# Decayed scores of HGRN and GLA in 64-row tiles of the array, written to two PSUM banks

## Chip, cores and metric

The kernel runs on one core of a Trainium2 chip. The metric is the device time of one execution in microseconds, as the median of several runs. A profiled execution of the same program gives the trace. TensorE's matmuls (PE) and its weight loads (PEld) are shown apart; VectorE is DVE, ScalarE ACT, GpSimd POOL, the DMA-issuing engine SP.

## What is computed

Two layers of a decoder. In each, one input projection feeds four groups of heads (retention, HGRN2, GLA, RWKV-7), their outputs go through one output projection, and cross-attention into 256 memory rows follows. It is done for a prompt of 2048 rows and for 8 x 8 sample rows. The change concerns HGRN2 and GLA, which are this recurrence (S is the state of one head, g the log of a decay per key channel):

```
def chunked_gated_linear(q, k, v, log_g, s0):
    """S_t = diag(exp g_t) S_{t-1} + k_t v_t^T, o_t = S_t^T q_t, evaluated chunkwise."""
    ...
    diff = b[:, :, :, None, :] - b[:, :, None, :, :]
    decay = jnp.where(causal, jnp.exp(jnp.minimum(diff, 0.0)), 0.0)
    scores = jnp.sum(qf[:, :, :, None, :] * kf[:, :, None, :, :] * decay, axis=-1)
    o = (jnp.einsum('bhjm,bhmv->bhjv', scores, vf)
         + jnp.einsum('bhjk,bhkv->bhjv', qf * jnp.exp(b), S))
```

HGRN has 4 heads of 64 key channels, GLA 4 heads of 32. All is float32.

## The kernel before

The prompt goes through each layer in four blocks of 512 rows. In a block come, in the order of the code: dense projections (groups of 12 or 24 matmuls, PSUM pool `psd`), RWKV in four units of 128 rows on the PSUM pools `psa` and `psc` in turn, GLA and HGRN in two half blocks of 256 rows each on the pool `psb` (two banks), retention, the gates (again dense groups), the output projection, cross-attention. A program orders the instructions of each engine once, before the run, by priorities that follow the code's order and the table `PRI`; `held` lifts eleven of twelve matmuls of a run so that a group stays together. Each engine then works through its own list in that order, so a matmul that waits holds up all that stand behind it.

`dyadic` (lines 670 to 740) makes the decayed scores of a half block. Scores between rows of one chunk of 128 are split by levels s = 1, 2, 4, ... 64: at level s, pairs of neighbouring runs of s rows are handled, the earlier run as keys, the later as queries. Between levels the keys of the earlier runs and the queries of the later runs are multiplied in place by the decay over the other run (`k_step`, `q_step`), so that each level is a plain product. The keys `k` lie with 128 channels on the partitions, which are two heads of HGRN (`NG` = 2, twice, `NC` = 2) or four of GLA (`NG` = 4, `NC` = 1). A matmul over all 128 partitions would add the heads up; so `apart` writes, for every product, `NG` copies of the level's queries into a tile `qx2` (two buffers), each masked to one head's channels (`hm2`, `hm4`). In the trace this tile is `qx`. `products` then takes 64 columns of `k` as weights and the masked copies as moving columns, into one PSUM bank of `psb`. The result is merged into the score tile `sT` by a multiplication with a mask (the two products of level 1) or by `copy_predicated` (levels 2 to 32, line 727); level 64 goes by ScalarE. `qk` of GLA shows as `dn_qk`, HGRN's queries and keys as `dn_hq` and `dn_hf`.

`outputs` (lines 605 to 668) multiplies queries by the state S and scores by the values into one bank, and updates S. GLA's state is a 128 x 256 tile: a 32 x 64 block for each of the four heads on the diagonal.

In the trace each float32 matmul of the code is two instructions, so a group that the code and the order give as 8 matmuls is 16 there.

Of the kernel before, what the change touches and what calls it, by code (L numbers as in the profile page):

```python
# [56 lines left out]
def shape_constants(seq, past):  # L57
    f = np.float32
    c = {}
# [43 lines left out]
    c["hm4"] = ((part // 32)[:, None] == np.arange(4)[None, :]).astype(f)  # L103
# [39 lines left out]
def decoder(ctx, tc, I, C, O):  # L143
# [461 lines left out]
    def outputs(seg, sT, v, qd, S, NG, NC, kT, tot, wp, eps, center, evac, state_out=None):  # L605

        P, nt = seg.P, seg.nt
        KD = 128 // NG
        if not seg.sample:
            po = PS("r").rearrange("p (t n) -> p t n", t=2)  # L610
            w = NG * 64
            for t in range(nt):
                for c in range(NC):
                    if center:
                        mm(po[:, t, c * w:(c + 1) * w], qd[:, c, t * 128:(t + 1) * 128], S[:, c, :], True, False)
                    else:
                        for e in range(2):
                            mm(po[64 * e:64 * e + 64, t, c * w:(c + 1) * w], qd[:, c, t * 128 + 64 * e:t * 128 + 64 * e + 64], S[:, c, :], True, False)
                    for g in range(NG):
                        h = c * NG + g  # L620
                        if center:
                            mm(po[:, t, h * 64:(h + 1) * 64], sT[:, t * NH + h].rearrange("p e n -> p (e n)"), v[:, t, h * 64:(h + 1) * 64], False, True)
                        else:
                            for e in range(2):
                                ep = slice(64 * e, 64 * e + 64)
                                mm(po[ep, t, h * 64:(h + 1) * 64], sT[:, t * NH + h, e, :], v[:, t, h * 64:(h + 1) * 64], False, True)
# [16 lines left out]
        for h in range(NH):  # L643
            c, g = divmod(h, NG)
            mm(pa[:SN, h * 64:(h + 1) * 64], sT[:SN, h, 0, :], v[:SN, 0, h * 64:(h + 1) * 64])
# [23 lines left out]

    def dyadic(seg, q, k, a, NG, NC, sT, wp):  # L670

# [3 lines left out]
        nh = P // 64  # L675
        m = nt * NC
        u = m * NG
        hm = K["hm%d" % NG]

        def apart(s, f):  # L680
            qx = wp.tile([128, NC, NG, n // 2], F32, name="qx2", tag="qx2", bufs=2)
            for c in range(NC):
                src = q[:, c].rearrange("p (b f s) -> p b f s", f=2, s=s)[:, :, f, :]
                shape = [128, NG, n // (2 * s), s]
                tt(V, qx[:, c].rearrange("p g (b s) -> p g b s", s=s), bc(src.unsqueeze(1), shape),
                   bc(hm.unsqueeze(2).unsqueeze(3), shape), ALU.mult)
            return qx

        def products(s, f):
            qx = apart(s, f)  # L690
            ps = PS("r")[:P, :u * 32].rearrange("p (i g n) -> p i g n", i=m, g=NG)
            for t in range(nt):
                for c in range(NC):
                    for e in range(nh):
                        b = t * nh + e
                        mm(ps[64 * e:64 * e + 64, t * NC + c], k[:, c, 64 * b:64 * b + 64], qx[:, c, :, 32 * b:32 * b + 32])
            out = sT[:P, :, 0, :].rearrange("p u (b f s) -> p u b f s", f=2, s=s)[:, :, :, f, :]
            return out, ps.rearrange("p i g (b s) -> p (i g) b s", s=s)
# [6 lines left out]
        def q_step(s, tot):  # L705
            qv = q.rearrange("p c (b f s) -> p c b f s", f=2, s=s)
            tv = tot.rearrange("p c (b f) -> p c b f", f=2)
            tt(V, qv[:, :, :, 1, :], qv[:, :, :, 1, :], bc(tv[:, :, :, 0:1], [128, NC, n // (2 * s), s]), ALU.mult)
# [4 lines left out]
        out, ps = products(1, 0)  # L713
        ev = K["I64"][:P].rearrange("p (b f) -> p b f", f=2)[:, :, 0:1]
        tt(V, out, ps, bc(ev.unsqueeze(1), [P, u, 32, 1]), ALU.mult)
        k_step(1, a)
        out, ps = products(1, 1)
        tt(V, out, ps, bc(K["pmask"][:P].unsqueeze(1).unsqueeze(3), [P, u, 32, 1]), ALU.mult)
        tt(V, q, q, a, ALU.mult)
        tot = q_step(1, a)  # L720
        for li, s in enumerate(seg.levels):
            if s == 1:
                continue
            if s < 64:
                out, ps = products(s, 1)
                mk = dmask[:P, li].rearrange("p (b s) -> p b s", s=s).unsqueeze(1)
                V.copy_predicated(out, bc(mk, [P, u, 32 // s, s]), ps)  # L727
            else:
                qx = apart(s, 1)
                A.activation(sT[64:128, :, 1, :], sT[64:128, :, 0, :], AF.Copy)  # L730
                G.memset(sT[64:128, :, 0, :], 0.0)
                ps = PS("r")[:, :NH * 64].rearrange("p (i g n) -> p i g n", i=NC, g=NG)
                for c in range(NC):
                    for t in range(nt):
                        mm(ps[64 * t:64 * t + 64, c], k[:, c, t * P:t * P + 64], qx[:, c, :, t * 64:(t + 1) * 64])
                for t in range(nt):
                    A.activation(sT[0:64, t * NH:(t + 1) * NH, 1, :], ps[64 * t:64 * t + 64].rearrange("p i g n -> p (i g) n"), AF.Copy)
            k_step(s, tot)
            tot = q_step(s, tot)
        return tot  # L740
# [28 lines left out]
    def R_gla(l, seg, st, d, on, wp):  # L769
# [16 lines left out]
        tot = dyadic(seg, qk[:, 0:1, :], qk[:, 1:2, :], a, 4, 1, sT, wp)  # L786
# [1209 lines left out]
```

## Time and profile before

| | us |
|---|---|
| median of 3 runs | 3726.42 |
| lowest, highest | 3723.85, 3737.66 |
| the profiled execution | 3730.45 |
| its span, first to last instruction | 3728.6 |

The profile is of one execution. Busy time counts an engine's instructions from start to end; matmuls overlap in the pipeline, so the length of one says little and the distance from a group's start to the start of the next group says how long it holds the engine. The chain of waits starts at the last instruction and goes back at each step to what released it.

### The profile page before, as it was taken

The numbers are of one execution on the slowest core, as the hardware profiler recorded it, in microseconds if no ns is written. First come the engines' busy times: TensorE is split into PE (matmuls) and PEld (weight loads), VectorE is DVE, ScalarE is ACT, GpSimd is POOL, SyncE is SP. The second block draws the span as 40 slices with busy tenths as digits, with TensorE's granted clock in tenths as the row PEclk, the third lists the DMA queues.
The fourth block names the chain that finished last, engine by engine and source line by source line (L and its number), as shares of the span: only waits on it lengthen the run. The fifth ranks groups of instructions, "written<-read, shape, count | busy, mean of one in ns | idle before, by whom it ended". The sixth has DMA issues, their size and how long they took to land.

```text
span 3728.6 us, 81858 instructions
## 1 busy us (share of the span) xinstructions
PE 3466.4 (93%) x32922; PEld 2850.0 (76%) x32922; DVE 2433.2 (65%) x7737; ACT 1387.9 (37%) x3425; POOL 569.9 (15%) x760
## 2 busy tenths in 40 slices
PE   7998799997999999999998888999889999999997
PEld 5767687786977888778876767877678878877787
DVE  4788545785437854786468865478744688547854
ACT  4442334422244324432434322443214342244323
POOL 3323331020000100110122233111200001000100
PEclk9999999998999999999999988999979999999999
DMA  6422674244662254325442246541545522542154
GB/s 189 140 103 78 188 233 180 69 124 151 206 209 92 74 188 153 109 72 182 167 160 89 85 131 209 188 145 67 152 150 180 178 84 89 188 167 82 71 187 183
DMA packets 244128, 530.48 MB, mean 142 GB/s; under 512 B 66982, under 2 KB 181926, under 8 KB 199718
## 3 DMA queue, kind: packets, MB, share of 16 engines
q1 hardware_dynamic: 243750, 525.25, 41.3%
q8 instruction: 260, 4.26, 0.5%
q14 instruction: 118, 0.97, 0.1%
HBM read 410.04 MB, written 115.16 MB: 141 GB/s over the span
## 4 chain that ended last, share of the span: by engine, by line
PE 69%; DVE 19%; issue 5%; ACT 4%; DMA 2%; POOL 2%; SPq 0%; POOLq 0%; ACTq 0%; DVEq 0%
PE psd L230 36%; PE psc L230 12%; PE psa L230 10%; PE psb L230 6%; DVE qx L236 2%; PE psa L272 2%; PE psc L272 2%; PE psb L272 2%; DVE rsq L236 1%; DVE Wb L911 1%; DVE Xb L911 1%; POOL whl L236 1%; DVE osb L236 1%; DVE dn_qk L236 1%; DVE sT L727 1%
## 5 line engine op out<-in xcount | busy, mean ns | idle before, releaser
L230 PE MATMUL psd<-act,whl 128*128 128x512 f32 (+1 forms) x4032 | 1015.4, 404 | 27.2 <-DVE th L1240 12.4
L230 PEld LDWEIGHTS psd<-act,whl 128*128 128x128 f32 (+1 forms) x4032 | 751.2, 191 | 207.5 <-issue 19.7
L230 PE MATMUL psd<-whl,act 128*128 128x256 f32 x3840 | 545.8, 293 | 5.4 <-POOL whl L236 4.8
L230 PEld LDWEIGHTS psd<-whl,act 128*128 128x128 f32 x3840 | 485.1, 193 | 36.0 <-issue 19.7
L236 POOL TENSOR_TENSOR whl<-wraw,whl 128x1024 fp32r<-128x1024 f32 (+1 forms) x90 | 217.9, 2426 | 385.4 <-ACT whl L358 383.3
L280 POOL TENSOR_TENSOR ri<-ri,mhalf 128x1 f32<-128x1 f32 (+1 forms) x87 | 49.1, 565 | 1097.8 <-DVE ri L279 1092.5
L230 PE MATMUL psd<-whl,oh 128*128 128x256 f32 x1152 | 211.9, 285 | 3.0 <-DMA whl<-w_w_out 3.0
L230 PEld LDWEIGHTS psd<-whl,oh 128*128 128x128 f32 x1152 | 177.5, 189 | 4.8 <-DMA whl<-w_w_out 3.9
L230 PE MATMUL psd<-whl,ol 128*128 128x256 f32 x576 | 162.8, 283 | 0.0
L913 ACT ACTIVATE Xb<-X 32x128 f32<-32x128 f32 x324 | 99.3, 307 | 156.0 <-DVE X L929 91.0
L358 ACT ACTIVATE whl<-wraw 128x1024 fp32r<-128x1024 f32 (+1 forms) x90 | 94.2, 1049 | 117.7 <-PE psa L230 38.3
L236 DVE TENSOR_TENSOR x<-x,psd 128x256 f32<-128x256 f32 x72 | 30.3, 421 | 136.9 <-PE psd L230 136.9
L236 DVE TENSOR_TENSOR qx<-dn_hq,fpack 128x256 f32<-128x256 f32 x256 | 109.1, 455 | 0.6
L230 PEld LDWEIGHTS psd<-whl,ol 128*128 128x128 f32 x576 | 108.5, 189 | 0.8 <-DVE ol L236 0.8
L230 PE MATMUL psb<-qx,dn_hf 128*64 128x64 f32 (+1 forms) x1920 | 95.5, 237 | 8.3 <-DVE qx L236 6.5
L1240 DVE SCALAR_TENSOR_TENSOR th<-th,psd 128x512 f32<-128x512 f32 x48 | 32.2, 685 | 104.4 <-ACT th L1239 104.4
L230 PEld LDWEIGHTS psb<-qx,dn_hf 128*64 128x64 f32 x1920 | 73.3, 141 | 35.0 <-issue 13.9
L435 ACT ACTIVATE xs<-xn 128x1024 f32<-128x1024 f32 (+1 forms) x34 | 35.8, 1054 | 166.8 <-PE psb L272 159.8
L230 PE MATMUL psb<-qx,dn_qk 128*64 128x128 f32 (+1 forms) x960 | 88.3, 295 | 3.0 <-DVE dn_qk L236 2.8
L236 DVE TENSOR_TENSOR qx<-dn_qk,fpack 128x512 f32<-128x512 f32 x128 | 88.2, 690 | 3.9 <-ACT dn_qk L1244 2.8
L727 DVE COPY_PREDICATED sT<-upack,psb 128x256 f32<-128x256 uint8 x160 | 78.8, 493 | 16.8 <-PE psb L230 14.5
L230 PE MATMUL psd<-hts,wraw 128*64 128x64 f32 x1984 | 85.1, 231 | 3.8 <-DVE th L1240 3.8
(759 smaller groups left out, 7516.6 us busy)
## 6 DMA issues: line engine op xcount, KB each, us to landing
whl<-w_w_out SPq DMA_DIRECT2D x56, 1024.0 KB
wraw<-in_w_in SPq DMA_DIRECT2D x76, 512.0 KB
wraw<-in_w_out SPq DMA_DIRECT2D x32, 512.0 KB
w_w_out<-whl SPq DMA_DIRECT2D x16, 1024.0 KB
x<-x SPq DMA_DIRECT2D x32, 512.0 KB
whl<-w_rw_r SPq DMA_DIRECT2D x12, 1024.0 KB
whl<-w_rw_k SPq DMA_DIRECT2D x12, 1024.0 KB
whl<-w_rw_v SPq DMA_DIRECT2D x12, 1024.0 KB
```

Of the source, the lines that this page charges most:

```text
L230: PE.matmul(out, lhsT=lhsT, rhs=rhs, start=start, stop=stop, skip_group_check=True)
L236: e.tensor_tensor(out, a, b, op)
L272: PE.transpose(out, in_, ident[:rows, :rows])
L280: G.tensor_tensor(y, y, mhalf[:P], ALU.pow)
L358: A.activation(hl[:, 0], raw, AF.Copy)
L435: A.activation(out, xt, AF.Square, accum_out=ss[:P])
L727: V.copy_predicated(out, bc(mk, [P, u, 32 // s, s]), ps)
L911: V.tensor_copy(o, i)
L913: A.activation(o, i, AF.Copy)
L1240: V.scalar_tensor_tensor(th, th, 1.0, x, ALU.add, ALU.mult)
```

## The change

Instead of masking the queries to one head for each product, a matmul takes only the 64 partitions that hold its heads: rows 0 to 63 (p = 0) and rows 64 to 127 (p = 1), each into a PSUM bank of its own. HGRN has one head in each 64 rows and needs no masked copy; the queries `q` are the moving operand themselves, read with a step that takes the level's runs. GLA has two heads in each 64 rows (`NP` = 2); its queries are copied twice with a mask (`hm32`), once for the first product and once after the first query step, and that second copy lives on: later steps multiply both copies, and `outputs` reads them. The two GLA heads of a half share a matmul of 64 moving columns and, in `outputs`, the columns of a state tile of 128 x 128. The score tile is ordered by halves, which `place` looks up.

```
-        u = m * NG
-        hm = K["hm%d" % NG]
-        def apart(s, f):
-            qx = wp.tile([128, NC, NG, n // 2], F32, name="qx2", tag="qx2", bufs=2)
+        w = m * NP
+        rows = [slice(64 * p, 64 * p + 64) for p in range(2)]
+        mine = lambda x, p: x[:, p * w:(p + 1) * w]
+        def apart(i):
+            if NP == 1:
+                return q.unsqueeze(2)
+            x = wp.tile([128, NC, NP, n], F32, name="qx2", tag="qx2", bufs=2)
             for c in range(NC):
...
+                tt(V, x[:, c], bc(q[:, c].unsqueeze(1), [128, NP, n]), bc(K["hm32"].unsqueeze(2), [128, NP, n]), ALU.mult)
+            return x
+        Q = [apart(0)]
...
         def products(s, f):
-            qx = apart(s, f)
-            ps = PS("r")[:P, :u * 32].rearrange("p (i g n) -> p i g n", i=m, g=NG)
+            v = Q[0].rearrange("p c g (b f s) -> p c g b f s", f=2, s=s)[:, :, :, :, f, :]
+            r = 32 // s
+            ps = [PS("r")[:P, :w * 32].rearrange("p (i n) -> p i n", i=m) for _ in range(2)]
             for t in range(nt):
                 for c in range(NC):
                     for e in range(nh):
                         b = t * nh + e
-                        mm(ps[64 * e:64 * e + 64, t * NC + c], k[:, c, 64 * b:64 * b + 64], qx[:, c, :, 32 * b:32 * b + 32])
+                        for p in range(2):
+                            mm(ps[p][64 * e:64 * e + 64, t * NC + c], k[rows[p], c, 64 * b:64 * b + 64], v[rows[p], c, :, r * b:r * b + r, :])
...
-        def q_step(s, tot):
+        def q_step(s, tot, x):
-            qv = q.rearrange("p c (b f s) -> p c b f s", f=2, s=s)
+            qv = x.rearrange("p c g (b f s) -> p (c g) b f s", f=2, s=s)
...
-                V.copy_predicated(out, bc(mk, [P, u, 32 // s, s]), ps)
+                for out, ps in products(s, 1):
+                    V.copy_predicated(out, bc(mk, [P, w, 32 // s, s]), ps)
...
-                        mm(ps[64 * t:64 * t + 64, c], k[:, c, t * P:t * P + 64], qx[:, c, :, t * 64:(t + 1) * 64])
+                        for p in range(2):
+                            mm(ps[p][64 * t:64 * t + 64, c], k[rows[p], c, t * P:t * P + 64], Q[0][rows[p], c, :, t * P + 64:t * P + 128])
...
-                for h in range(NH):
-                    c, g = divmod(h, NG)
-                    gs = slice(g * KD, (g + 1) * KD)
-                    blk = S[gs, c, g * 64:(g + 1) * 64]
-                    V.scalar_tensor_tensor(blk, blk, tot(t, c)[gs], pu[gs, c, :], ALU.mult, ALU.add)
+                for c in range(NC):
+                    for p in range(2):
+                        gs = slice(64 * p, 64 * p + 64)
+                        blk = S[gs, c, p * 64:(p + 1) * 64]
+                        V.scalar_tensor_tensor(blk, blk, tot(t, c)[gs], pu[gs, c, :], ALU.mult, ALU.add)
...
-        st["gla"] = stp.tile([128, 1, 256], F32, name="S_gla", tag="S_gla")
+        st["gla"] = stp.tile([128, 1, 128], F32, name="S_gla", tag="S_gla")
```

TensorE's list in HGRN's second half block, third block of the first layer, before (`psd<-act,whl` are the gates' dense groups; a row gives output, weights and moving operand or the reverse, the output's shape and the count):

```order
L230 MATMUL psb<-qx_15190,dn_hf 64x64 x8
L230 MATMUL psb<-qx_15207,dn_hf 64x64 x8
L230 MATMUL psd<-act,whl 128x512 x12
L230 MATMUL psb<-qx_15224,dn_hf 64x64 x8
L230 MATMUL psd<-act,whl 128x512 x12
L230 MATMUL psb<-qx_15241,dn_hf 64x64 x8
```

and the same products after:

```order
L230 MATMUL psb<-dn_hq,dn_hf 64x32 x16
L272 MATMUL psa<-fpack,osb 128x128 x4
L230 MATMUL psd<-act,whl 128x512 x12
L230 MATMUL psb<-dn_hq,dn_hf 64x32 x16
L272 MATMUL psa<-fpack,dn_rk 128x128 x4
L230 MATMUL psd<-act,whl 128x512 x12
L230 MATMUL psb<-dn_hq,dn_hf 64x32 x16
```

Twice as many matmuls of half the columns; a dense group stands between any two products now, where the first two stood side by side.

TensorE's list in GLA's first half block of the same block, before (`Xb`, `Wb`, `X` belong to RWKV):

```order
L230 MATMUL psb<-qx_14434,dn_qk 64x128 x4
L272 MATMUL psa<-fpack,X 128x128
L230 MATMUL psd<-act,whl 128x512 x12
L230 MATMUL psa<-Xb,XB 32x128 x4
L230 MATMUL psc<-Wb,XB 32x128 x4
L230 MATMUL psb<-qx_14446,dn_qk 64x128 x4
```

and after, where `qx_14773` is GLA's lasting second copy:

```order
L230 MATMUL psb<-qx_14773,dn_qk 64x64 x8
L272 MATMUL psc<-fpack,X 128x128
L230 MATMUL psc<-Xb,XB 32x128 x4
L230 MATMUL psd<-act,whl 128x512 x12
L230 MATMUL psa<-Wb,XB 32x128 x4
L230 MATMUL psc<-Wb,XB 32x128 x4
L230 MATMUL psb<-qx_14773,dn_qk 64x64 x8
```

Four matmuls of 128 columns became eight of 64; RWKV's two units stand further on in the list at the same product.

VectorE's list in HGRN's second half block, before (`rsq`, `hri` are a norm of another part):

```order
L727 COPY_PREDICATED sT<-upack,psb 128x8x8x4
L236 TENSOR_TENSOR dn_hf<-dn_hf,tot_15222 128x2x32x4
L236 TENSOR_TENSOR qx_15258<-dn_hq,fpack 128x256 x2
L292 SCALAR_TENSOR_TENSOR hri<-rsq,hri 128x8
L537 SCALAR_TENSOR_TENSOR gs<-psd,cols_101,gs 128x511
L236 TENSOR_TENSOR dn_hq<-dn_hq,tot_15256 128x2x8x16
```

and after:

```order
L745 COPY_PREDICATED sT<-upack,psb 128x4x8x4 x2
L236 TENSOR_TENSOR dn_hf<-dn_hf,tot_15731 128x2x32x4
L236 TENSOR_TENSOR dn_hq<-dn_hq,tot_15731 128x2x32x4
L236 TENSOR_TENSOR sT<-psa,fpack 128x2x128
L745 COPY_PREDICATED sT<-upack,psb 128x4x4x8 x2
```

The eviction became two, the masks `qx` went, and the query step moved from two levels ahead of the key step (`tot_15256` beside `tot_15222`) to right behind it, at the same level.

## Rows read from the trace of the kernel before

**Rows 1.** The page: busy time by engine; shares of the chain by line.

```profile
PE 3466.4 (93%) x32922; PEld 2850.0 (76%) x32922; DVE 2433.2 (65%) x7737; ACT 1387.9 (37%) x3425; POOL 569.9 (15%) x760
...
PE psd L230 36%; PE psc L230 12%; PE psa L230 10%; PE psb L230 6%; DVE qx L236 2%; PE psa L272 2%; PE psc L272 2%; PE psb L272 2%; DVE rsq L236 1%; DVE Wb L911 1%; DVE Xb L911 1%; POOL whl L236 1%; DVE osb L236 1%; DVE dn_qk L236 1%; DVE sT L727 1%
```

**Rows 2.** Windows (stretch, length, busy by engine): sum of sixteen GLA and HGRN stretches; one stretch.

```profile
sum 1583.00, PE 1507.74 PEld 1196.35 DVE 1300.58 ACT 598.05 POOL 259.76; mean PE 94.23 PEld 74.77 DVE 81.29 ACT 37.38 POOL 16.23
...
1300.00:1325.00 25.00, 24.73 (x240) 19.90 (x238) 23.59 (x71) 6.34 (x11) 3.32 (x7) 1.00 0.49 168
```

**Rows 3.** Timeline of PE (start us, length us, what) in HGRN's second half block.

```profile
1308.28 0.69 PE L230 MATMUL psb<-qx,dn_hf 128*64 128x64 f32 x16
1308.89 3.02 PE L230 MATMUL psd<-act,whl 128*128 128x512 f32 x12
```

**Rows 4.** Timeline of PE in GLA's half blocks: a product, the last level.

```profile
1186.21 0.66 PE L230 MATMUL psb<-qx,dn_qk 128*64 128x128 f32 x8
1186.80 1.70 PE L230 MATMUL psd<-whl,act 128*128 128x256 f32 x12
...
1153.69 0.65 PE L230 MATMUL psb<-qx,dn_qk 128*64 128x256 f32 x4
1154.28 0.33 PE L272 MATMUL psa<-fpack,X 128*128 128x128 f32 x1
```

**Rows 5.** Timeline of PE and PEld: sixteen 64x64 matmuls on two and on four quarters.

```profile
1185.19 0.85 PEld L230 LDWEIGHTS psc<-Z,XT 64*64 64x64 f32 x16
1185.19 1.09 PE L230 MATMUL psc<-Z,XT 64*64 64x128 f32 x16
...
148.53 0.42 PEld L230 LDWEIGHTS psa<-ar,kp 64*64 64x64 f32 x16 [0.33 <-issue]
148.53 0.67 PE L230 MATMUL psa<-ar,kp 64*64 64x128 f32 x16
...
149.12 0.44 PE L272 MATMUL psc<-fpack,dn_v 128*128 128x128 f32 x2
```

**Rows 6.** Timeline of PE: eight matmuls of 2 and of 64 columns, and what follows.

```profile
1200.06 0.40 PE L230 MATMUL psa<-fpack,wt 128*64 128x2 f32 x8
1200.38 1.33 PE L230 MATMUL psd<-whl,act 128*128 128x256 f32 x9
...
1328.68 0.40 PE L230 MATMUL psb<-dn_hv,sT 128*64 128x64 f32 x8
1328.91 0.39 PE L230 MATMUL psb<-S_hgrn,dn_hq 128*64 128x128 f32 x4
...
1329.36 0.40 PE L230 MATMUL psb<-dn_hv,ha 128*64 128x64 f32 x8
1329.69 2.56 PE L230 MATMUL psd<-act,whl 128*128 128x512 f32 x10
```

**Rows 7.** Groups by line and shape on DVE: busy us, mean ns, idle before.

```profile
L236 DVE TENSOR_TENSOR qx<-dn_hq,fpack 128x256 f32<-128x256 f32 x256 | 109.1, 455 | 0.6
L236 DVE TENSOR_TENSOR qx<-dn_qk,fpack 128x512 f32<-128x512 f32 x128 | 88.2, 690 | 3.9 <-ACT dn_qk L1244 2.8
L727 DVE COPY_PREDICATED sT<-upack,psb 128x256 f32<-128x256 uint8 x160 | 78.8, 493 | 16.8 <-PE psb L230 14.5
...
L635 DVE SCALAR_TENSOR_TENSOR S_gla<-S_gla,tot,psb 32x64 f32<-32x64 f32 x128 | 35.4, 277 | 3.9 <-PE psb L230 1.4
...
L929 DVE COPY_PREDICATED X<-upack,psa 128x128 f32<-128x128 uint8 x64 | 19.2, 300 | 25.4 <-PE psa L230 24.5
```

**Rows 8.** Timeline of DVE in HGRN's second half block: one link between two products.

```profile
1309.97 0.42 DVE L727 COPY_PREDICATED sT<-upack,psb 128x256 f32<-128x256 uint8 x1
1310.30 0.41 DVE L236 TENSOR_TENSOR dn_hf<-dn_hf,tot 128x256 f32<-128x256 f32 x1
```

**Rows 9.** Windows: the third block of the first and of the second layer.

```profile
1118.00:1498.00 380.00, 370.63 (x3485) 307.24 (x3484) 252.17 (x852) 137.08 (x351) 32.73 (x62) 1.00 0.37 130
...
2962.00:3345.00 383.00, 367.54 (x3433) 303.38 (x3428) 261.28 (x834) 147.04 (x368) 31.91 (x64) 0.98 0.38 132
```

More of the change, by code (lines that the diff above doesn't have):

```diff
@@ L102, in shape_constants @@
     c["hm2"] = ((part // 64)[:, None] == np.arange(2)[None, :]).astype(f)
-    c["hm4"] = ((part // 32)[:, None] == np.arange(4)[None, :]).astype(f)
+    c["hm32"] = ((part // 32 % 2)[:, None] == np.arange(2)[None, :]).astype(f)
     c["pmask"] = ((part % 64 // 2)[:, None] == np.arange(32)[None, :]).astype(f)
@@ L603, in expand, with outputs @@
         return vx[:SN].rearrange("p b d -> p (b d)")
-    def outputs(seg, sT, v, qd, S, NG, NC, kT, tot, wp, eps, center, evac, state_out=None):
+    def outputs(seg, sT, at, v, qd, S, NG, NC, kT, tot, wp, eps, center, evac, state_out=None):
         P, nt = seg.P, seg.nt
         KD = 128 // NG
+        NP = NG // 2
         if not seg.sample:
             po = PS("r").rearrange("p (t n) -> p t n", t=2)
-            w = NG * 64
+            p5 = po.rearrange("p t (c g j d) -> p t c g j d", c=NC, g=2, j=NP)
+            es = [slice(0, 128)] if center else [slice(0, 64), slice(64, 128)]
             for t in range(nt):
                 for c in range(NC):
[L614 to L626, printed above, removed]
+                    for j in range(NP):
+                        for e in es:
+                            mm(p5[e, t, c, :, j, :], qd[:, c, j, t * 128 + e.start:t * 128 + e.stop], S[:, c, :], True, False)
+                        for g in range(2):
+                            h = c * NG + g * NP + j
+                            x = sT[:, at(t, h)].rearrange("p e n -> p (e n)")
+                            for e in es:
+                                mm(po[e, t, h * 64:(h + 1) * 64], x[:, e], v[:, t, h * 64:(h + 1) * 64], False, True)
                 pu = PS("r")[:, :NC * 64].rearrange("p (c n) -> p c n", c=NC)
@@ L668, in outputs, with place, at @@
         state_out()
+    def place(NG, NC, nt):
+        NP = NG // 2
+        def at(t, h):
+            c, g = divmod(h, NG)
+            p, j = divmod(g, NP)
+            return ((p * nt + t) * NC + c) * NP + j
+        return at
     def dyadic(seg, q, k, a, NG, NC, sT, wp):
@@ L711, in q_step @@
             return new
-        out, ps = products(1, 0)
         ev = K["I64"][:P].rearrange("p (b f) -> p b f", f=2)[:, :, 0:1]
-        tt(V, out, ps, bc(ev.unsqueeze(1), [P, u, 32, 1]), ALU.mult)
+        for out, ps in products(1, 0):
+            tt(V, out, ps, bc(ev.unsqueeze(1), [P, w, 32, 1]), ALU.mult)
         k_step(1, a)
-        out, ps = products(1, 1)
-        tt(V, out, ps, bc(K["pmask"][:P].unsqueeze(1).unsqueeze(3), [P, u, 32, 1]), ALU.mult)
+        for out, ps in products(1, 1):
+            tt(V, out, ps, bc(K["pmask"][:P].unsqueeze(1).unsqueeze(3), [P, w, 32, 1]), ALU.mult)
         tt(V, q, q, a, ALU.mult)
-        tot = q_step(1, a)
+        tot = q_step(1, a, q.unsqueeze(2))
+        Q[0] = apart(1)
         for li, s in enumerate(seg.levels):
@@ L724, in dyadic @@
             if s < 64:
[L725 removed]
                 mk = dmask[:P, li].rearrange("p (b s) -> p b s", s=s).unsqueeze(1)
[L727 removed]
+                for out, ps in products(s, 1):
+                    V.copy_predicated(out, bc(mk, [P, w, 32 // s, s]), ps)
             else:
[L729 removed]
                 A.activation(sT[64:128, :, 1, :], sT[64:128, :, 0, :], AF.Copy)
                 G.memset(sT[64:128, :, 0, :], 0.0)
[L732 removed]
+                ps = [PS("r")[:, :NC * NP * 64].rearrange("p (c g n) -> p c g n", c=NC, g=NP) for _ in range(2)]
                 for c in range(NC):
                     for t in range(nt):
[L735 removed]
+                        for p in range(2):
+                            mm(ps[p][64 * t:64 * t + 64, c], k[rows[p], c, t * P:t * P + 64], Q[0][rows[p], c, :, t * P + 64:t * P + 128])
                 for t in range(nt):
[L737 removed]
+                    for p in range(2):
+                        o = mine(sT[0:64], p)[:, t * NC * NP:(t + 1) * NC * NP, 1, :]
+                        A.activation(o, ps[p][64 * t:64 * t + 64].rearrange("p c g n -> p (c g) n"), AF.Copy)
             k_step(s, tot)
[L739 to L740 removed]
+            tot = q_step(s, tot, Q[0])
+        if seg.sample and NP > 1:
+            tt(V, q, Q[0][:, :, 0], Q[0][:, :, 1], ALU.add)
+        return Q[0], tot
     def sample_state(src, nm, wp, KD):
@@ L808, in R_hgrn @@
         sT = wp.tile([128, seg.nt * NH, seg.P // 64, 64], F32, name="sT", tag="sT")
-        tot = dyadic(seg, q, f, a, 2, 2, sT, wp)
+        qd, tot = dyadic(seg, q, f, a, 2, 2, sT, wp)
+        at = place(2, 2, seg.nt)
         kT = totok(f, 2, seg, wp, "ha", 256)
@@ L845, in R_ret @@
         sT = wp.tile([128, seg.nt * NH, seg.P], F32, name="sT", tag="sT")
+        at = lambda t, h: t * NH + h
         for t0 in range(0, nt, step):
```

33 lines of the change are left out of this document (16 added, 17 removed).

## The prediction

> **What bounds the kernel now.** I read the page's busy table first, then the chain, then the stretches that the change touches, then single groups of matmuls inside them. TensorE is busy for 3466 of 3728.6 us, VectorE for 2433 [rows 1]; the chain that ends last runs for 36% of the span through the dense groups of `psd`, for 6% through the matmuls of `psb` and for 2% through the masked queries `qx` [rows 1]. The sixteen stretches in which GLA's and HGRN's half blocks run last 1583 us together; TensorE is busy for 1508 us of them and VectorE for 1301 [rows 2]. So TensorE has 75 us of idle time there to give back, no more; everything else must come from its own work getting shorter. That decides the method: I price the change by how long TensorE is held by each group of matmuls, from the start of the group to the start of the next one on the engine, and give VectorE's relief only a place in the range.
>
> Four readings carry the sum. An HGRN product (16 matmul instructions of 128 rows by 64 weight columns, 64 moving columns; each matmul of the code is two in the trace) holds TensorE for 0.61 us: 1308.28 to 1308.89 [rows 3]. A GLA product (8 of them, 128 moving columns) holds it for 0.59 us: 1186.21 to 1186.80 [rows 4]. The same sixteen 64x64 matmuls of 128 columns take 1.02 us where two quarters of the array are used (`Z,XT`, 1185.19 to 1186.21) but 0.59 us (`ar,kp`, 148.53 to 149.12) where the code walks through all four [rows 4, 5]. There the sixteen weight loads took 0.42 us of PEld time, not 0.85 [rows 5]: four loads and four matmuls do go abreast. And eight matmuls of only 2 columns still hold TensorE for 0.32 us, as many as eight of 64 columns do (0.33 us) [rows 6]: below 64 columns the weight load sets the pace, some 0.058 us for each round of loads that go abreast ((0.61 - 0.33) / 4 more rounds of two).
>
> **GLA's scores.** A product goes from 8 instructions of 128 columns on two tiles to 16 of 64 columns on four: 4 rounds in either case, but a round falls from 128 columns to 64. Eight 64-column matmuls in four rounds take 0.33 us after a group of the same tile shape [rows 6]; HGRN's group, entered from another shape, is 0.61 - 8 x 0.058 = 0.15 us above its rounds, so 4 x 0.058 + 0.15 = 0.38 us, and I take 0.39 for the two extra starts. That saves 0.20 us on 7 products x 16 half blocks = 112: **-22 us**. Ends: 0.33 us would save 29, and 0.59, the sixteen `ar,kp` of twice the columns, nothing. At the last level GLA's 4 instructions of 256 columns hold TensorE for 0.59 us [rows 4]; afterwards 8 of 128 columns in two rounds: 0.59 - 2 x 0.107 (`ar,kp`'s group less two of its four rounds of 128 columns, a round being (1.02 - 0.16) / 8) = 0.38 us, **-3 us** over 16.
>
> **HGRN's scores.** 16 instructions of 64 columns become 32 of 32 columns, on four tiles instead of two: again 8 rounds. The columns halve, but the loads don't get shorter and there are twice as many, so the round stays at the load's pace: 0.61 us becomes 0.59, **-2 us** over 112 (ends: -4, and +52 if the loads don't go abreast, a rival below). The last level, 8 instructions of 128 columns, becomes 16 of 64 columns as a GLA product does: 16 x 0.20, **-3 us**. The queries are now read with a step (every other element at the first levels); if that halved the rate, 32 columns would cost what 64 do and stay under the load's pace, and GLA's first three products would lose 0.2 us each, +10 us; no row shows such a read, and I take 0.
>
> The Trainium skill has a rule that speaks against just this: TensorEngine Tiling (Array Packing), Instruction Overhead, says that a matmul of one column takes as long as one of 60 and that one shouldn't tile away a dimension that is already small. The 0.32 us of the 2-column group [rows 6] agree with it; by it HGRN wins nothing on TensorE, which is also what my sum says, as long as four go abreast.
>
> **Changes of tile shape.** The same 8 matmuls hold TensorE for 0.23 us when the next group has their tile shape (1328.68 to 1328.91) and for 0.33 us when a 128x128 group follows (1329.36 to 1329.69) [rows 6]: leaving a shape costs 0.10 us. The new products have RWKV's 64x64 shape. Counted along TensorE's order, the shape changes 2135 times before and 1994 times after: 141 x 0.10 = **-14 us** (ends: 0, if those exits stood in idle time, and -14). The interchunk products of GLA go from 4 instructions of 256 columns per tile row to 8 of 128: the same columns, loads under them, 0.
>
> **VectorE.** Removed: HGRN's 256 masks, 109.1 us, and GLA's 128, 88.2 us, of which 32 stay (22.1) [rows 7]. Added: each eviction of 128x256 becomes two of 128x128, 160 x (2 x 0.300 - 0.493) = 17.1 us, and as much apiece for the 64 of level 1, 6.8; GLA's query steps work on two copies, 128 elements more, half of what a mask of 512 elements costs over one of 256: 96 x (0.690 - 0.455) / 2 = 11.3. GLA's state takes 64 updates fewer, -17.7 us [rows 7]. Net -158 of 2433 us. ScalarE, at 37%, gets 64 evictions more [rows 1]. None of it is in the sum: TensorE was held anyway. What VectorE's relief can give is a part of the 75 us; a third, -25, is my lower end.
>
> **A new wait.** Masked copies let the queries run ahead: `qx` of the next level was made while TensorE worked, and from a product to the next there stood one eviction and the step on the keys (0.33 + 0.42 us: 1309.97, 1310.30) [rows 8]. Now TensorE reads the queries themselves, so their step waits for the product, and the next product waits for it; both banks of the pool `psb` are in use at each level, so both evictions stand before it too. The link grows by 0.42 for the query step and 2 x 0.30 - 0.42 = 0.18 for the evictions: 0.60 us, on 7 links x 32 half blocks = 224, 134 us if none of it were covered. What covers it is the group of twelve dense matmuls that stands between two products, 3.0 us in HGRN's second half [rows 3], 1.6 us elsewhere (1186.80) [rows 4]; the new order keeps such a group between nearly all of them. I put it at 0.
>
> **Sum.** -22 - 3 - 2 - 3 - 14 = -44 us on the profiled run's own 3730.45 us (span 3728.6), 3686. The median of the three runs, 3726.42, is 4.0 us under that run, so I forecast 3682 us.
>
> **Rivals.** (1) The order eats the gain. The instruction counts move every place in it: the lane of GLA and HGRN stands later against RWKV's, and in the first layer's third block 108 instead of 132 of the gates' matmuls are left behind the last HGRN product to fill TensorE. Two blocks of the same work, the third of each layer, leave TensorE idle for 9.4 and 15.5 us [rows 9]: 6 us a block by order alone, 17 us over eight if the signs differ, 48 if not. A loss of 15 to 40 gives 3697 to 3722; I name 3712, no change. (2) The new wait shows. From 73 uncovered links of 224 (44 / 0.60) the kernel is no faster, from 104 it is slower by 0.5%; for it speaks that 28 of HGRN's 112 products are split into 14 matmuls and 2 that follow up to 16 rows later, and that VectorE is busy for 23.6 of 25 us in such a stretch [rows 2]; against it the dense groups. With half of the links bare: 3682 + 67 = 3749, slower. (3) The four tiles don't go abreast when a matmul has only 32 columns, each pair of loads costing its 0.058: HGRN's product 0.61 + 0.46, +52 us; GLA's 0.39 becomes 0.61, +2 against before; with -14, 3726 + 40 = 3766, slower. `ar,kp` speaks against it, but its 128 columns hide the loads.
>
> **How the numbers follow.** The forecast, 3645 to 3707, has 0.61; below it 0.04 (shape changes, a larger part of VectorE's relief). Rival 1 has 0.17, rival 2 0.11, rival 3 0.07. A measurement of this kernel tells 0.5% (18.6 us) from no change: faster, under 3707.8, 0.65; within, to 3745, 0.18; slower 0.17. The range, 3645 to 3750, leaves out 0.04 below and rival 3 with half of rival 2 above, 0.16 in all.
>
> **What would show it.** Right: a GLA product holding TensorE for about 0.39 us, an HGRN product for about 0.59; VectorE's busy time near 2275 us; TensorE's idle time in these stretches not above 75 us. Wrong: HGRN products near 1 us (rival 3); waits of TensorE for the query or key steps, and products following their predecessor by a bare link (rival 2); the single groups as forecast, yet more idle time in RWKV's stretches or behind the last HGRN product (rival 1).

## The result, and the profile after

The kernel after takes 3625.94 us in the median of four runs (3621.8 to 3635.8), the kernel before 3727.24; the ratio is 0.9726 [0.9714, 0.9737]. The gain is 101 us where 44 were forecast, and the time lies below the lower end of the range, 3645. The page after, busy time by engine and the chain by line, answers to [rows 1]:

```profile
PE 3419.7 (94%) x35978; PEld 2842.5 (78%) x35978; DVE 2283.1 (63%) x7543; ACT 1393.4 (38%) x3489; POOL 562.1 (16%) x760
...
PE psd L230 39%; PE psc L230 12%; PE psa L230 11%; PE psb L230 5%; PE psc L272 2%; PE psa L272 2%; PE psb L272 2%; DVE rsq L236 1%; DVE Wb L936 1%; DMA wraw<-in_w_in 1%; POOL whl L236 1%; ACT Xb L938 1%; DVE hss L561 1%; DVE sT L745 0%; DVE osb L236 0%
```

The span fell by 105.2 us, from 3728.6 to 3623.4. TensorE's busy time gave 46.7 of it (3466.4 to 3419.7), about the forecast sum of 44. The other 58.5 is idle time of TensorE, and nearly all of it went where the prediction had not looked. It counted the sixteen stretches of GLA and HGRN [rows 2]; the eight stretches from the last output of HGRN to the output projection, which hold retention and the gates, come behind them. Windows of those stretches, before (the second block, and the sum of all eight; stretch, length, busy time of PE, PEld, DVE, ACT and POOL with counts, granted clock, DMA share, GB/s):

```profile
846.10:942.00 95.90, 76.20 (x641) 62.41 (x640) 51.05 (x155) 23.30 (x48) 6.07 (x8) 0.84 0.50 158
...
sum 598.80, PE 499.30 PEld 408.07 DVE 347.82 ACT 176.13 POOL 87.47; mean PE 62.41 PEld 51.01 DVE 43.48 ACT 22.02 POOL 10.93
```

and after:

```profile
829.00:900.00 71.00, 69.00 (x605) 57.18 (x600) 45.79 (x138) 23.62 (x49) 2.29 (x4) 1.00 0.67 217
...
sum 447.20, PE 403.91 PEld 335.55 DVE 274.60 ACT 146.91 POOL 62.16; mean PE 50.49 PEld 41.94 DVE 34.32 ACT 18.36 POOL 7.77
```

Idle time there was 598.8 - 499.3 = 99.5 us and is now 447.2 - 403.9 = 43.3: 56 of the 58.5 us. What TensorE waited for shows in its timeline before, second block (in brackets the idle time and what ended it; `xs` is a normed row of another part, `osb` retention's output):

```profile
881.77 0.63 PE L272 MATMUL psb<-fpack,xs 128*128 128x128 f32 x4 [3.48 <-DVE xs L439]
885.30 1.09 PE L272 MATMUL psc<-fpack,osb 128*128 128x128 f32 x4 [2.91 <-DVE osb L236]
...
904.58 1.09 PE L272 MATMUL psc<-fpack,osb 128*128 128x128 f32 x4 [6.81 <-DVE osb L236]
```

and after, where the first half's transposes wait for the same norm:

```profile
845.04 0.63 PE L272 MATMUL psc<-fpack,osb 128*128 128x128 f32 x4 [0.23 <-DVE osb L236]
...
853.48 5.73 PE L230 MATMUL psd<-act,whl 128*128 128x512 f32 x24
```

The norm of `osb` is a chain of small VectorE instructions, some 6 us long. After, dense groups of the gates stand between the outputs and their transposes; before, from 897 us on, the list has none of them there. I measure this by a count: of the 240 dense matmuls of a block's gates, how many still stand in TensorE's list behind retention's first output. Before it is 120, 108, 228, 240, 120, 96, 204, 240 in the eight blocks; after it is 192, 180, 240, 240, 180, 96, 240, 240. In the first, second and fifth block, whose counts rose by 60 to 72, the idle time fell by 13.2, 17.7 and 8.6 us, 39.5 of the 56. It also fell by 7.1 us in the seventh (204 to 240) and by 7.5 in the sixth, whose count did not change.

TensorE's own 46.7 us, as the time it was held by each kind of group (start to the next start, without idle time, summed): GLA's products -24.9, GLA's outputs and state products -16.0, HGRN's products and outputs +6.5, retention -11.4, transposes -7.2, all else +6.2. Retention was not changed; before, part of it ran at a lower granted clock behind those waits:

```profile
886.00:904.00 18.00, 11.09 (x62) 9.93 (x60) 8.76 (x29) 3.46 (x6) 0.00 (x0) 0.50 0.00 0
```

0.50 is the lower of the clock's two levels, 1.2 GHz, behind the two waits of 3.48 and 2.91 us. In the kernel after the stretch from 829 to 900 us has 1.00. Over the whole kernel the clock gave nothing, though: by the clock records of the two traces TensorE was busy at the lower level for 183 us before and for 182 after. What retention and the transposes won there other groups lost, among them the outputs of HGRN, whose +3.0 is 2.5 us of clock.

Single groups after, to be set beside [rows 3] and [rows 4], in TensorE's timeline (GLA's product, then HGRN's, each with the group behind it):

```profile
1083.31 0.46 PE L230 MATMUL psb<-qx,dn_qk 64*64 64x64 f32 x16
1083.70 0.44 PE L272 MATMUL psa<-fpack,dn_v 128*128 128x128 f32 x2
...
1262.81 0.67 PE L230 MATMUL psb<-dn_hq,dn_hf 64*64 64x32 f32 x32
1263.41 0.66 PE L272 MATMUL psa<-fpack,dn_rk 128*128 128x128 f32 x4
```

0.39 and 0.60 us, as forecast.

### The profile page after: what moved, and what is told of

It reads as the page before. It is cut to its first block, busy times and chain, and to the rows that moved or that the text cites. A ratio compares the mean times of both kernels' runs of the same rounds, so it can differ in the third digit from the quotient of the medians.

```text
span 3623.4 us, 87919 instructions
## 1 busy us (share of the span) xinstructions
PE 3419.7 (94%) x35978; PEld 2842.5 (78%) x35978; DVE 2283.1 (63%) x7543; ACT 1393.4 (38%) x3489; POOL 562.1 (16%) x760
## 4 chain that ended last, share of the span: by engine, by line
PE 73%; DVE 14%; ACT 5%; issue 4%; DMA 2%; POOL 1%; SPq 0%; POOLq 0%; ACTq 0%; DVEq 0%
PE psd L230 39%; PE psc L230 12%; PE psa L230 11%; PE psb L230 5%; PE psc L272 2%; PE psa L272 2%; PE psb L272 2%; DVE rsq L236 1%; DVE Wb L936 1%; DMA wraw<-in_w_in 1%; POOL whl L236 1%; ACT Xb L938 1%; DVE hss L561 1%; DVE sT L745 0%; DVE osb L236 0%
## 5 line engine op out<-in xcount | busy, mean ns | idle before, releaser
L745 DVE COPY_PREDICATED sT<-upack,psb 128x128 f32<-128x128 uint8 x320 | 92.5, 326 | 41.7 <-PE psb L230 38.2
L230 PE MATMUL psb<-dn_hq,dn_hf 64*64 64x32 f32 (+1 forms) x3840 | 101.5, 226 | 7.2 <-DVE dn_hq L236 3.2
L230 PEld LDWEIGHTS psb<-dn_hq,dn_hf 64*64 64x64 f32 x3840 | 83.8, 139 | 31.3 <-issue 17.8
L230 PEld LDWEIGHTS psd<-hts,wraw 128*64 128x64 f32 x1984 | 69.9, 140 | 20.0 <-issue 10.5
L230 PE MATMUL psa<-whl,oh 128*128 128x256 f32 x448 | 82.8, 283 | 0.0
L230 PE MATMUL psc<-whl,oh 128*128 128x256 f32 x448 | 82.7, 283 | 0.0
```

Of the source, the lines that this page charges most:

```text
L230: PE.matmul(out, lhsT=lhsT, rhs=rhs, start=start, stop=stop, skip_group_check=True)
L745: V.copy_predicated(out, bc(mk, [P, w, 32 // s, s]), ps)
```

## The experiments

Each run is given by its median and its ratio to the kernel before, with a 95% interval.

**One half of the change alone.** First GLA as after and HGRN with its masked copies, then the reverse.

```
-        qd, tot = dyadic(seg, q, f, a, 2, 2, sT, wp)
-        at = place(2, 2, seg.nt)
+        tot = dyadic_masked(seg, q, f, a, 2, 2, sT, wp)
+        qd = q.unsqueeze(2)
+        at = lambda t, h: t * NH + h
```

> The kernel after, with HGRN's scores made by the masked copies of the kernel before; GLA as changed. TensorE's own time: GLA's products and outputs were held for 41 us less in the kernel after than before (products 25, outputs and state products 16). What differs is the idle time of TensorE between the last HGRN output and the output projection, 99.5 us before and 43.3 after. Theory A (the order: retention's waits are covered only where its first outputs stand ahead of more than 120 of the gates' 240 matmuls): in this order the counts are 156, 144, 132 to 240, 240, 144, 96, 204, 238 against 120, 108, 228, 240, 120, 96, 204, 240 before, so idle time falls a little, by 5 to 20 us: 3665 to 3682. Rival B (each microsecond taken off VectorE gives back its share): GLA takes 64 of the 158 us, so 23 of the 56 us: 3663.

3665.88 us, ratio 0.9831 [0.9815, 0.9848]. TensorE was held 44 us less (products -25.2, outputs -15.9), and the idle time behind HGRN fell from 99.5 to 75.0: the lower end of theory A's range, and 3 us from B's number, so the time does not tell them apart. The idle time does: it fell by 24.5 us, where B said 23 and A 5 to 20.

> The kernel before, with HGRN's scores in 64-row tiles and two banks as in the kernel after; GLA masked as before. TensorE's own time: HGRN's products were held 3.5 us longer in the kernel after, so nothing to win there but the tile-shape exits, at most 7 us. Theory A (order): the counts of gate matmuls left at retention's first outputs are 120, 120, 216, 240, 156, 96, 192, 240, nearly those of before, so the idle time stays near 95 us: 3712 to 3727. Rival B (VectorE's relief by itself): HGRN takes 94 of the 158 us, so 33 of the 56 us: 3690.

3695.79 us, 0.9904 [0.9885, 0.9924]: between the theories, nearer to B. TensorE's busy time fell by 4 us only, but the idle time behind HGRN by 31.8 to 67.7, near the 33 of B and not the 4 or so of A. Only in the fifth block did the count rise much (120 to 156), and that block gave 11.8 us. The count is a sign and no law. The two spans fell by 64 and 34 us, together nearly the 105 of the whole. By these two runs the idle time could go in proportion to VectorE's relief; the next ones leave that relief as it is and move the order.

**The order alone.** In the kernel after, retention ranks 200 later (`wk4` is its pool; it had no entry):

```
-PRI = {'wkf': -4890, 'wk2': -223, ...}
+PRI = {'wkf': -4890, 'wk2': -223, ..., 'wk4': 200}
```

> The kernel after with one number of the order's table changed: retention's half blocks rank 200 later, so that their first outputs stand behind all but 96 of the gates' matmuls in all eight blocks (192, 180, 240, 240, 180, 96, 240, 240 in the kernel after). No work is added and VectorE keeps its relief. Theory A (order): every block gets the 17 to 26 us of idle time that the blocks with 96 to 120 had before: 8 x 20 = 160 us against 43, so 3626 + 115 = 3740, about the kernel before or slower. Rival B (VectorE's relief itself): the norms of retention come early enough with a free VectorE, within 20 us: 3626 to 3646.

3747.64 us, 1.0049 [1.0031, 1.0067]: theory A. All work of the change is in, VectorE has its relief, and one number takes more than the whole gain. The windows of its eight stretches (second block, third block, sum):

```profile
851.10:944.60 93.50, 76.13 (x611) 63.92 (x606) 47.98 (x141) 23.67 (x49) 2.70 (x4) 0.84 0.51 165
1327.60:1391.30 63.70, 48.87 (x225) 40.31 (x222) 36.90 (x101) 17.64 (x31) 2.31 (x4) 0.68 0.32 108
...
sum 618.30, PE 490.66 PEld 411.13 DVE 340.12 ACT 172.56 POOL 66.75; mean PE 61.33 PEld 51.39 DVE 42.52 ACT 21.57 POOL 8.34
```

Idle time 127.6 us, 14.8 to 18.4 in every block. TensorE's busy time rose from 3420 to 3463 us with the same matmuls, and by the clock records it was busy at the lower level for 272 us instead of 182: 43 us of slower clock beside 84 more of idle time, half a microsecond for each.

The other way round, the kernel before with GLA ranked 200 later (`'wk2': -23`), all masks in:

> The kernel before with one number of the order's table changed: GLA's half blocks rank 200 later. All masks stay, and VectorE has all its work. The counts of gate matmuls left at retention's first outputs become 144, 192, 228, 234, 144, 96, 204, 228 (before 120, 108, 228, 240, 120, 96, 204, 240). Theory A (order): the second block's idle time after HGRN falls from 19.7 to 2 to 4 us, the first's and fifth's from 17.4 and 21.2 to 9 to 14, together 24 to 34 us, and each microsecond of idle time brings up to half of another by the slower clock behind it: 3727 - 24 to 45, so 3682 to 3703. Rival B (VectorE's relief itself, by its time in the run): nothing is relieved, 3720 to 3735.

3699.60 us, 0.9923 [0.9900, 0.9945]: theory A. Its second block and the sum of the eight stretches:

```profile
860.20:935.20 75.00, 72.88 (x627) 60.26 (x624) 47.66 (x140) 23.89 (x50) 3.25 (x4) 1.00 0.68 219
...
sum 509.40, PE 442.24 PEld 358.95 DVE 305.44 ACT 162.59 POOL 77.97; mean PE 55.28 PEld 44.87 DVE 38.18 ACT 20.32 POOL 9.75
```

The second block's idle time is 2.1 us instead of 19.7, the sum 67.2; retention and transposes were held 23 us less (19 in the kernel after), with no change to them. So the order can take such waits away without any relief of VectorE. A smaller step on the kernel after (`'wk2': -323`):

> The kernel after with one number of the order's table changed: GLA's half blocks rank 100 earlier. The counts at retention's first outputs stay in six blocks and fall in the second (180 to 120) and the seventh (240 to 180). Theory A (order): the second block's idle time rises from 2.0 to 11 to 17 us, the seventh's by up to 4, with the slower clock behind it 9 to 28 us in all: 3635 to 3654. Rival B: VectorE's work is the same, so the time is: 3621 to 3631.

3635.26 us, 0.9743 [0.9727, 0.9759]: theory A, at its lower edge. The ratio's interval overlaps that of the kernel after, so the time alone decides nothing here; but in the trace the second block's idle time went from 2.0 to 11.3, the seventh's from 0.0 to 3.8, the two blocks that were named.

**VectorE's work put back.** Masked copies that nobody reads, ahead of each product:

```
+            if not seg.sample:
+                extra(s, f)
```

> The kernel after, and beside it VectorE makes masked copies again that nobody reads: HGRN's 256 of 256 elements a partition, as before, and 112 of 512 for GLA. TensorE's program of matmuls is that of the kernel after in kind and count. If the change paid by TensorE's time alone (the sum of the prediction), the time stays near that of the kernel after, 3626 to 3640. If 55 of the 101 us came by way of VectorE's time, in whichever way, it goes back to about 3680. The counts of gate matmuls at retention's first outputs fall from 192, 180, 240, 240, 180, 96, 240, 240 to 96, 120, 204, 240, 96, 96, 228, 234, so theory A expects the idle time after HGRN near 95 us again.

3771.78 us, 1.0110 [1.0093, 1.0126], 92 us above what either theory gave. 75 and 50 us of the loss lie in the first and the fifth block (544 and 563 us from output projection to output projection, 469 and 513 after), in which GLA's scores now stand behind most of RWKV; the other six cost 17 together. GLA's extra tile may have delayed its pool; that was not tried by itself. Cleaner is the run with HGRN's masks alone, in a tile that has its place:

> The kernel after, and beside it VectorE makes HGRN's 256 masked copies (109 us of its time before) that nobody reads, in tiles that have their place already; nothing is added for GLA. Unlike the run with all masks kept, the order stays as it is: the counts of gate matmuls at retention's first outputs are 180, 180, 240, 240, 168, 96, 228, 240 against 192, 180, 240, 240, 180, 96, 240, 240. Theory A (the 55 us of idle time and clock came by the order alone): 3626 to 3645, since the six blocks with unchanged order cost 17 us in the run with all masks kept. Rival B (VectorE's time itself): 109 of the 158 us relieved are back, so 39 of the 56 us of idle time and some 15 of the slower clock: 3665 to 3680.

3666.24 us, 0.9835 [0.9807, 0.9862]: B's number, but not B's place. Windows from one output projection to the next, first, second and fourth block, after:

```profile
0.00:469.30 469.30, 417.17 (x4665) 336.84 (x4666) 318.51 (x1008) 191.21 (x445) 153.26 (x147) 0.93 0.46 151
469.30:900.00 430.70, 414.75 (x4454) 346.00 (x4452) 278.86 (x959) 166.28 (x420) 69.42 (x93) 0.98 0.47 155
...
1320.60:1715.80 395.20, 384.23 (x3971) 323.00 (x3970) 249.52 (x858) 147.56 (x383) 34.46 (x76) 0.99 0.38 135
```

and with HGRN's masks:

```profile
0.00:493.30 493.30, 415.29 (x4669) 335.05 (x4670) 336.20 (x1040) 190.22 (x444) 152.62 (x147) 0.93 0.45 144
493.30:938.10 444.80, 422.71 (x4450) 353.25 (x4449) 291.61 (x991) 166.43 (x421) 70.36 (x93) 0.95 0.46 150
...
1358.70:1754.20 395.50, 383.62 (x3973) 323.04 (x3972) 260.79 (x890) 147.29 (x383) 35.61 (x76) 0.99 0.38 134
```

VectorE (the third busy time) has 6 to 18 us more in every block. In the third to the eighth block that costs 0.0, 0.3, 1.5, 0.2, 1.0 and -0.2 us: nothing. In the first two it costs 24 and 14. In the first, the idle time behind HGRN rose from 4.2 to 16.7 with the count nearly unchanged (192 to 180). One of its waits can be followed, that for the norm of retention's first half: TensorE's transposes, then the first and the last step of that norm in VectorE's timeline,

```profile
443.43 1.08 PE L272 MATMUL psa<-fpack,osb 128*128 128x128 f32 x4 [5.18 <-DVE osb L236]
...
429.57 0.67 DVE L555 TENSOR_REDUCE hst<-osb 128x8 f32<-128x512 f32 x1
442.61 0.68 DVE L236 TENSOR_TENSOR osb<-osb,hri 128x512 f32<-128x512 f32 x1
```

and the same two steps in the kernel after:

```profile
410.98 0.69 DVE L555 TENSOR_REDUCE hst<-osb 128x8 f32<-128x512 f32 x1
416.41 0.69 DVE L236 TENSOR_TENSOR osb<-osb,hri 128x512 f32<-128x512 f32 x1
```

The norm took 13.7 us instead of 6.1, and 48 dense matmuls between the outputs and the transposes did not cover it, where 36 do after. No mask stands in this norm (VectorE made that block's last one for HGRN before 379 us); ten steps of the gates and of another norm do, two steps took 1.76 and 2.82 us, and why those two were so slow is not shown. So this wait came with VectorE's list, which had moved, and not with a mask ahead of it. In the second block the idle time behind HGRN stayed at 2.0; 6 us of idle time ahead of HGRN's last output and 8 of TensorE's busy time are not explained. So the relief from HGRN's masks is worth nothing in six blocks, and what part of the loss in the first two is the masks' own time stays open.

**The cut by twelve.** In the kernel before one line, at the state products:

```
                 pu = PS("r")[:, :NC * 64].rearrange("p (c n) -> p c n", c=NC)
+                run[2] = None
```

> The kernel before with one line more: in the outputs the count of twelve, by which matmuls are kept together, begins anew at the four state products, so that the fourteen matmuls of 128 rows of GLA are cut into 10 and 4 and no longer into 12 and 2. GLA's state products held TensorE for 17.6 us before and 8.1 after, its outputs for 40.5 and 34.1. Theory: this fall of 16 us comes from the cut (twelve matmuls a row after, so that none is cut), and so 10 us or more of it come back here with the masks kept; the count of gate matmuls at retention's first outputs rises in the fifth block (120 to 168), worth 8 us of idle time there: 3727 - 18 = 3709, not above 3717. Rival: it comes from the tile shape of the groups beside them; then the state products stay at 17.6 us and the time at 3720 to 3732.

3685.95 us, 0.9878 [0.9861, 0.9896]: the theory held, and the gain was more than twice the forecast. GLA's state products were held 8.0 us instead of 17.6, its outputs 34.8 instead of 40.5: 15.3 us, what the kernel after has. TensorE's timeline before (two cuts inside one row's products):

```profile
1159.18 0.30 PE L230 MATMUL psb<-dn_gv,gmn 128*32 128x64 f32 x2
1159.41 0.33 PE L230 MATMUL psb<-dn_gv,sT 128*64 128x64 f32 x2
1159.67 0.30 PE L230 MATMUL psb<-dn_gv,gmn 128*32 128x64 f32 x2
1159.90 0.68 PE L230 MATMUL psb<-dn_gv,sT 128*64 128x64 f32 x14
```

and here:

```profile
1166.78 0.29 PE L230 MATMUL psb<-dn_gv,gmn 128*32 128x64 f32 x8
1167.00 3.01 PE L230 MATMUL psd<-act,whl 128*128 128x512 f32 x12
```

Eight in a row hold TensorE for 0.22 us; two by themselves 0.23. The other 30 us are the rest of an order that moved everywhere: idle time -17, and dense groups and retention -13, which were at the higher clock for longer (TensorE was busy at the lower level for 149 us instead of 183).

**The order of the tiles in a product.** First the halves of the rows outside, so that neighbours use two quarters of the array:

```
-            for t in range(nt):
-                for c in range(NC):
-                    for e in range(nh):
-                        b = t * nh + e
-                        for p in range(2):
+            for p in range(2):
+                for t in range(nt):
+                    for c in range(NC):
+                        for e in range(nh):
+                            b = t * nh + e
```

> The kernel after with the loops of a product turned: all tiles of rows 0 to 63 first, then all of rows 64 to 127, so that neighbouring matmuls use two quarters of the array and not four. The same matmuls, the same evictions; the counts at retention's first outputs are about the same (192, 180, 234, 240, 192, 108, 240, 240). Theory: four go abreast in the kernel after, and only that keeps an HGRN product at 0.60 us. Here its 32 instructions take sixteen rounds, 0.15 + 16 x 0.058 = 1.08 us, and GLA's sixteen take eight, 0.61: 112 x (0.48 + 0.24) = 81 us, 3707 if none of it lies in time that was idle, and not under 3670. Rival: the rounds form by themselves in any order of issue: 3620 to 3632.

3631.28 us, 0.9733 [0.9718, 0.9748]: the rival. A product of HGRN took 0.62 us in the median, GLA's 0.40. Then both halves outside (`p`, `e`, `t`, `c`), eight instructions in a row on one quarter:

> The kernel after with the loops of a product turned so that eight matmul instructions in a row fall on the same quarter of the array (rows 0 to 63 and the first 64 columns, then its other columns, then rows 64 to 127). Same matmuls, and TensorE's list is the same group by group. First theory, of the prediction (what counts is how many tiles go abreast): an HGRN product takes 32 loads one behind the other, at half of a round's 0.058 at the least, 0.15 + 32 x 0.029 = 1.08 us against 0.60, and GLA's 0.61 against 0.39: 3626 + 79 = 3705, and not under 3665. Second theory, from the run with two quarters (a 64x64 load or 32 columns hold TensorE for 0.015 us wherever they stand): 0.60 to 0.63 us, 3622 to 3634.

3656.83 us, 0.9804 [0.9786, 0.9823]: neither. HGRN's product took 1.11 us, so its products were held 51.3 us longer, which the first theory gave for them; GLA's took 0.41. Timelines, two quarters and then one:

```profile
1262.04 0.69 PE L230 MATMUL psb<-dn_hq,dn_hf 64*64 64x32 f32 x32
1262.65 1.70 PE L230 MATMUL psd<-whl,act 128*128 128x256 f32 x12
```

```profile
1273.69 1.18 PE L230 MATMUL psb<-dn_hq,dn_hf 64*64 64x32 f32 x32
1274.80 0.66 PE L272 MATMUL psa<-fpack,dn_rk 128*128 128x128 f32 x4
```

Two quarters in turn are enough for 32 columns, one is not. The span grew by only 26.5 us: GLA's products were held 2.7 us longer too, but dense groups 10.6 us less, other groups 8, and 9 us of idle time went. The work of these others is the same; TensorE was busy at the lower clock for 148 us instead of 182. Why is not shown.

**A faster version.** The products of the kernel after are cut too; here the count is sixteen inside them.

```
+            run[0], run[2] = 16, None
...
+            run[0], run[2] = DENSE, None
```

> The kernel after, in which the count of twelve is sixteen inside a product of scores and begins anew at it, so that a product's sixteen matmuls are no longer cut into 14 and 2 or 12 and 4 (102 whole HGRN products in TensorE's list instead of 75). The counts of gate matmuls at retention's first outputs stay (192, 180, 234, 240, 168, 96, 228, 240). Theory: a cut costs TensorE one more entry and exit, 0.15 us, and lets the product's end wait behind up to 16 rows of other work; 27 cuts less give 4 us of TensorE's time and as much again of links: 3618 to 3623. Rival: the cuts lie where TensorE had other work, and only the first of it counts: 3622 to 3628.

3626.31 us, 0.9722 [0.9706, 0.9737], the rival, and no change: HGRN's products were held 6.0 us less and TensorE 10.5 in all, and 9.4 us of idle time took their place. Next the sample rows' retention and gates one block later:

```
-TURN = {'rwkv': 0, 'gla': 0, 'hgrn': 1, 'ret': 1, 'gate': 1, 'end': (1, 1)}
+TURN = {'rwkv': 0, 'gla': 0, 'hgrn': 1, 'ret': 2, 'gate': 2, 'end': (2, 2)}
```

> The kernel after with the sample rows' retention and gates in the third block of a layer instead of the second. Theory A (order): retention's counts become 192, 240, 192, 240, 180, 144, 192, 240; the sixth block, which had 96 and 19.0 us of idle time after HGRN, falls to 9 to 14, the third and seventh lose some cover (240 to 192) but stay where idle time was under 8: 3612 to 3624. Rival: the sample rows' work brings its waits into the block that it is moved to, and nothing is gained: 3624 to 3636.

3617.73 us, 0.9692 [0.9674, 0.9709], as theory A: the sixth block's idle time behind HGRN fell from 19.0 to 7.0. Both edits:

> The two edits together, uncut products and the sample rows' retention in the third block; counts 192, 240, 204, 240, 168, 144, 180, 240. By theory the sum of both, 3606 to 3620; if each is worth nothing, 3624 to 3634.

3603.23 us, 0.9656 [0.9641, 0.9671]: 23 us below the kernel after, the fastest here, and 3 below the range given. And with the sample rows' GLA in the second block:

> As the run with both edits, and the sample rows' GLA in the second block instead of the first. Counts 210, 192, 204, 240, 234, 96, 180, 240: the fifth block, 12.6 us of idle time in the kernel after, gets full cover (168 to 234), the sixth falls back to 96. Theory A: fifth block -9 us, sixth +6 against the run with both edits: within 6 us of it. Rival: as the run with both edits plus the waits of sample rows in the second block, up to 15 us more.

3642.79 us, 0.9762 [0.9745, 0.9778]: the rival, and more. The fifth block kept 13.0 us of idle time with a count of 234, the first got 8.6 with 210, the sixth went back to 20.0. Theory A fails for the fifth block; a high count doesn't cover every wait.

## Why the prediction was wrong

The sign was right and the sum for TensorE's own time came out near (46.7 us against 44), in part by luck, as its terms show. The size was wrong, since more than half of the gain was priced at nothing.

- **What bounds the kernel.** The step that failed is "TensorE has 75 us of idle time there to give back, no more; everything else must come from its own work getting shorter". It is true of the sixteen stretches: 84.6 us before, 83.6 after, measured from their first score to HGRN's last output. But the order does not end with them. The 99.5 us behind them were in the trace before, 17 to 26 us in each of the first two blocks of both layers, and no term and no bound looked at them.
- **Rival 1** named the mechanism and bounded it wrongly. It took the third blocks as its measure [rows 9], whose counts before were 228 and 204, and gave the order only a loss. Behind HGRN 56 us of idle time went, and with it 19 us of clock in retention and the transposes, which other groups lost again. The run with retention late (+122) and the run of before with GLA later (-32) show that the order alone can move as much and more, beside a sum of 44. How the 56 us divide between the order and VectorE's relief is not shown: the runs with one half of the change lost idle time nearly in proportion to the relief, while with HGRN's masks put back only 17 us of it came back, where 39 were expected by that rival.
- **GLA's scores**: -25 forecast, -24.9 measured, with some luck. The price of a round, 0.058 us, does not follow from the working beside it: (0.61 - 0.33) / 4 is 0.07, which gives 0.33 us for a product and -29. The 0.39 us that was forecast is what was measured.
- **HGRN's scores**: -5 forecast, +3.5 measured, +3.0 in the outputs behind them, most of that +3.0 by the clock. Whole products took 0.60 us as forecast. Products that the count of twelve cuts took more: in the run that keeps more of them whole they were held 6.0 us less together.
- **Changes of tile shape**: -14 forecast. GLA's outputs and state products, priced at 0 apart from that term, fell by 16.0, and the run that undid the cut alone gave 15.3 with the old scores. The count of 141 exits met the size by luck, and named the wrong cause: twelve matmuls a row fit the count of twelve.
- **VectorE**: 2283 us, 2275 forecast. The relief was given "a third" of the 75 us as the lower end. In the sixteen stretches it gave 1 us; behind them its part is open, except that HGRN's masks cost nothing in six blocks of eight.
- **Rival 3** was a real price, 51 against the 52 us given, and did not come due because neighbouring matmuls use different quarters. The reading of [rows 5] behind the sum, four abreast, fell for 32 and 64 columns: two quarters gave nearly the same time.
- **Rival 2**, the new wait, hardly showed. The groups by shape of the kernel after (busy us, mean ns, idle time just ahead and what ended it) have 6.1 + 5.1 us of idle time ahead of the products of levels 1 to 32; before it was 7.1 + 1.6:

```profile
L230 PE MATMUL psb<-dn_hq,dn_hf 64*64 64x32 f32 x3584 | 93.5, 225 | 6.1 <-DVE dn_hq L236 2.1 <-DVE carry L539 1.3 <-issue 1.1
L230 PE MATMUL psb<-qx,dn_qk 64*64 64x64 f32 x1792 | 58.4, 230 | 5.1 <-DVE qx L236 2.0 <-DVE dn_qk L236 1.6 <-DVE sT L236 1.0
```

## What to carry to other kernels

Where instructions are put in order by priority, an edit's price is not only its own groups. Look at the stretches behind it for latency chains (here a norm of many small steps), and at what dense work the new list leaves to cover them; that can be read from the list before any run. It is a sign only: a chain also grows when other work stands among its steps in its own engine's list. Groups kept together by a count should have a length that the count divides. And a wait of a few microseconds on TensorE is priced with the slower clock behind it.

## What the runs showed of the hardware

Behind two waits of 3.48 and 2.91 us TensorE's granted clock was 0.50 in a stretch of 18 us; over the run with retention late the lower clock cost 43 us beside 84 of idle time. Thirty-two instructions of 32 columns on 64x64 tiles take 0.60 us on four quarters in turn, 0.62 on two, and 1.11 with eight in a row on one. The Trainium skill, TensorEngine Tiling (Array Packing), Key Properties, says that different tiles load and multiply in parallel; the step from one quarter to two agrees with it, and from two to four little more came (0.62 to 0.60 us). Sixteen instructions of 64 columns took 0.41 us with four in a row on a quarter, 0.39 without, so there one quarter was no bound; why is open.
